# P·V products of 256 columns, a reordered output projection with kept weights, and a second block group in the down projection

## The chip, the cores and the metric

The kernel runs on one core of a Trainium2 chip. The metric is device time in microseconds (us): 2593.43 is the median of three runs of the kernel before (2592.44 to 2593.51). PE is the matrix engine (TensorE), PEld its weight loads, DVE the vector engine, ACT the scalar engine, POOL the gpsimd engine, SP the queue that issues most loads.

## What is computed

A trunk of two layers on 16 learned and 1024 input frames (T = 1040), width 1024, everything in float32:

```python
for i in range(DEPTH):
    xn = rms_norm(h, attn_norm[i])
    gq, gk, gv, gr, glr, fq, fk, fv, ff = split(xn @ w_in[i])
    o_gla = rms_norm(gla_chunk_causal(gq / 8, gk, gv, log_a), gla_norm[i]) * silu(gr)
    o_fox = rms_norm(forgetting_attention(fq, fk, fv, log_f), fox_norm[i])
    h = h + concatenate([o_gla, o_fox]) @ w_out[i]
    h = h + conv_ffn(rms_norm(h, ffn_norm[i]), w_up[i], conv_w[i], conv_b[i], w_down[i])
return rms_norm(h, final_norm)[:, 16:]

def conv_ffn(x, w_up, conv_w, conv_b, w_down):
    u, g = split(causal_conv3(x @ w_up, conv_w) + conv_b)
    return (silu(g) * u) @ w_down
```

`forgetting_attention` is a causal softmax attention with eight heads of 64 columns and a bias from a cumulated forget gate. The gated width D_FF is 22 tiles of 128.

## The kernel before

The hidden state stands transposed: eight tiles of 128 features by 1040 frames. PE multiplies in a 32-bit format with a shorter fraction, so each operand is split into a high part (ACT casts it) and a low part (DVE subtracts), and one product takes three matmuls (`mm3`, lines 218 to 220). The split of weights is `weights` (L179 loads, L185 is the caller of the cast `hi`, L187 the subtraction `lo`) and, for block products, `up_split` (L1028, L1029); that of activations is L332 and L333.

A layer has these stages. *Attention* (forget-gate heads, `fox`): queries go in groups of one or two tiles of 116, keys in tiles of 116 too. For each pair of key chunk and query tile the exponentials P are transposed on PE (`fox_transposes`, L690) into one bank, split into `PT` (high and low part beside each other for each of four key tiles), and `fox_av` (L708) multiplies them by V: one matmul per key tile and part, 232 columns wide for two query tiles and 116 on the diagonal. Products of the next head's projections fill PE in between.

*Output projection* (`wout` in `ffn_up`): the frames are done in two halves `h` of 520 (layer 1: 524 and 516), each in 36 x 2 x 3 = 216 matmuls; eight output tiles `m` in the orders (4, 0, 5, 1, 6, 2, 7, 3) and (0, 4, 1, 5, 2, 6, 3, 7). Tiles 0 to 3 were done for seven of the eight inputs during attention, so they take 6 matmuls and tiles 4 to 7 take 48. Banks rotate over four pairs by `i % 4`. Weights are loaded and split one tile ahead, once for each half. Each tile's result is added to the residual h (DVE, L1110), squared (ACT, L1116) and summed into `acc` (DVE, L1117). `scale` sums `acc` over partitions with a matmul by ones into a bank `ssq` of pair 3 (L1086), which DVE reads (L1089), and makes the factor of the norm (`rsqrt`, L273 to L277). In the second half, after the second tile, `scale(0)` and then the normed operands of the up projection are made among the remaining tiles (L1094, L1052, L1053); `gt` and `dd` (L1121, L1123) are the scaled differences between halves.

*Up projection*: block products with seven instead of eight multiplications on 2 x 2 blocks (weights by input halves and output tiles, activations by frame halves), in the order of the list `seq`; numbers p = 1 to 7 name the products, which share banks a, x and y and accumulate on them.

*Down projection* (`ffn_down`): the 22 gated tiles come back from DRAM (`actd`) and go in groups, `GROUPS` and `LAST`. A group "n" or "r" is plain: for eight output tiles, two halves, its tiles, two column pieces of 260 (layer 1: 256), three matmuls. "n" copies the result to a buffer `do` (ACT, L1462) and adds it to `hm` in DRAM by an accumulating DMA of POOL (L1464); "r" adds it on DVE to residual tiles that `load_residual` has loaded from `hm` (L1435). A group "s" is done by seven block products (`down_blocks`), for four pairs j of output tiles, in the order 2, 6, 5, 7, (j+1's 1), 4, 3 behind the first: bank a is copied by ACT after products 1, 6, 7 and 4 (L1376), x and y are added by DVE (L1375), and the sums `du` and `dg` go to `hm` by accumulating DMA (L1390, L1394). `prepare` is a generator that loads, splits and combines the operands of coming groups; `pump` takes steps of it between products while enough buffers ("slots" of 1040 columns, first in, first out) are free. *Last group* (`down_last`): three gated tiles in column chunks of 400, 384 and 256 over eight single banks; its result is added to the residual (L1538), squared, and is the next layer's input.

PE's order is that of the program in the stages behind attention; all other engines, and PE in attention, are ordered by a scheduler. Waits are in order on each engine, and on SP's and POOL's queues.

## Time and profile before

| | us |
|---|---|
| median of three runs | 2593.43 |
| the profiled run | 2591.4 |
| its span, first to last instruction | 2589.6 |
| output projection, layer 0 (first matmul to the first of the up projection) | 538.9 to 600.9 |
| up projection, layer 0 | 600.9 to 1048.1 |
| down projection, groups, layer 0 | 1048.1 to 1258.6 |
| last group of layer 1, final norm | 2537.3 to 2589.6 |

The trace is of one execution. A row of a timeline has start and duration (us), engine, line, operation, output<-inputs, shape, count, and in brackets how long the engine was idle before it and what ended that. A row of a group has the count, the busy time and the mean duration in ns, then the idle time before its instructions and who ended it. Matmuls overlap, so what one costs is the distance between starts, not the duration.

### The profile page before, as it was taken

The numbers are of one execution on the slowest core, as the hardware profiler recorded it, in microseconds if no ns is written. First come the engines' busy times: TensorE is split into PE (matmuls) and PEld (weight loads), VectorE is DVE, ScalarE is ACT, GpSimd is POOL, SyncE is SP. The second block draws the span as 40 slices with busy tenths as digits, with TensorE's granted clock in tenths as the row PEclk, the third lists the DMA queues.
The fourth block names the chain that finished last, engine by engine and source line by source line (L and its number), as shares of the span: only waits on it lengthen the run. The fifth ranks groups of instructions, "written<-read, shape, count | busy, mean of one in ns | idle before, by whom it ended". The sixth has DMA issues, their size and how long they took to land.

```text
span 2589.6 us, 48743 instructions
## 1 busy us (share of the span) xinstructions
PE 2495.7 (96%) x19278; PEld 2424.9 (94%) x19278; DVE 1786.6 (69%) x3494; ACT 1288.4 (50%) x2745; POOL 432.6 (17%) x598
## 2 busy tenths in 40 slices
PE   8999999898999999999999999999999999999997
PEld 7988999898999999999999899998899999999997
DVE  7656776759877777853665666776697777777535
ACT  7336666635544445641443565665464444455312
POOL 4033334310000000100301233332100000001002
PEclk9999999999999999999999999999999999999998
DMA  3132134342322223863312222143423222257721
GB/s 125 65 89 60 51 93 127 109 145 89 110 75 87 79 79 129 200 165 107 110 50 67 72 78 76 57 146 114 148 70 114 78 74 86 76 162 179 196 61 67
DMA packets 119670, 263.03 MB, mean 102 GB/s; under 512 B 15008, under 2 KB 32672, under 8 KB 119440
## 3 DMA queue, kind: packets, MB, share of 16 engines
q1 hardware_dynamic: 95136, 184.89, 22.8%
q0 software_dynamic: 22432, 72.71, 10.1%
q8 instruction: 151, 2.47, 0.4%
q10 hardware_dynamic: 1872, 2.31, 0.3%
q14 instruction: 79, 0.65, 0.1%
HBM read 179.26 MB, written 67.81 MB: 95 GB/s over the span
## 4 chain that ended last, share of the span: by engine, by line
PE 62%; issue 16%; DVE 13%; ACT 4%; DMA 3%; POOL 1%; SPq 0%; DVEq 0%; POOLq 0%; ACTq 0%
PE mm L218 7%; PE mm L220 6%; PE mm L219 6%; PE up L218 5%; PE up L219 5%; PE up L220 5%; PE down L218 5%; PE down L219 5%; PE down L220 5%; PE av L708 2%; DVE S L657 2%; PE tr L690 2%; ACT P L669 1%; PE wo L218 1%; PE wo L219 1%
## 5 line engine op out<-in xcount | busy, mean ns | idle before, releaser
L218 PE MATMUL up<-x,hi 128*128 128x260 f32 (+1 forms) x2464 | 697.3, 283 | 2.3 <-ACT x L1052 1.6
L220 PE MATMUL up<-x,hi 128*128 128x260 f32 (+1 forms) x2464 | 695.8, 282 | 2.2 <-DVE x L1053 2.2
L219 PE MATMUL up<-x,lo 128*128 128x260 f32 (+1 forms) x2464 | 696.1, 283 | 0.8 <-DVE lo L1029 0.8
L220 PEld LDWEIGHTS up<-x,hi 128*128 128x128 f32 x2464 | 465.5, 189 | 3.1 <-DVE x L1053 3.1
L218 PEld LDWEIGHTS up<-x,hi 128*128 128x128 f32 x2464 | 464.4, 188 | 3.4 <-ACT x L1052 2.2
L219 PEld LDWEIGHTS up<-x,lo 128*128 128x128 f32 x2464 | 464.8, 189 | 1.0 <-DVE lo L1029 1.0
L1029 DVE TENSOR_TENSOR lo<-raw,hi 128x512 fp32r<-128x512 f32 x364 | 249.0, 689 | 171.3 <-ACT hi L1028 171.3
L218 PE MATMUL mm<-xh,hi 128*128 128x348 f32 (+4 forms) x1056 | 364.6, 345 | 0.0
L220 PE MATMUL mm<-xl,hi 128*128 128x348 f32 (+4 forms) x1056 | 340.1, 322 | 0.0
L219 PE MATMUL mm<-xh,lo 128*128 128x348 f32 (+4 forms) x1056 | 339.2, 321 | 0.0
L1028 ACT CAST hi<-raw 128x512 fp32r<-128x512 f32 x364 | 224.5, 620 | 145.0 <-PE up L220 87.4
L185 ACT CAST hi<-raw 128x512 fp32r<-128x512 f32 (+2 forms) x192 | 112.4, 587 | 201.4 <-PE down L220 114.2
L218 PEld LDWEIGHTS mm<-xh,hi 128*128 128x128 f32 x1056 | 200.2, 190 | 5.9 <-issue 5.3
L219 PEld LDWEIGHTS mm<-xh,lo 128*128 128x128 f32 x1056 | 200.1, 190 | 0.4 <-issue 0.3
L220 PEld LDWEIGHTS mm<-xl,hi 128*128 128x128 f32 x1056 | 198.9, 188 | 0.3 <-issue 0.3
L219 PE MATMUL down<-ah,lo 128*128 128x260 f32 (+1 forms) x704 | 198.6, 282 | 0.3 <-DVE lo L187 0.3
L220 PE MATMUL down<-al,hi 128*128 128x260 f32 (+1 forms) x704 | 198.3, 282 | 0.0
L218 PE MATMUL down<-ah,hi 128*128 128x260 f32 (+1 forms) x704 | 198.3, 282 | 0.0
L669 ACT ACTIVATE P<-S,m 116x460 f32<-116x460 f32 (+2 forms) x224 | 124.8, 561 | 100.1 <-DVE m L657 97.9
L333 DVE TENSOR_TENSOR PT<-tr,PT 116x464 fp32r<-116x464 f32 (+3 forms) x240 | 123.0, 516 | 63.2 <-ACT PT L332 62.3
L1222 POOL DMA_DIRECT2D actd<-cv x44 | 23.6, 535 | 763.5 <-DVE cv L1221 742.5
L1011 DVE TENSOR_TENSOR raw<-raw,raw 128x512 f32<-128x512 f32 x198 | 129.9, 689 | 22.4 <-DMA raw<-in_wd_dram 18.4
(276 smaller groups left out, 5901.0 us busy)
## 6 DMA issues: line engine op xcount, KB each, us to landing
raw<-in_wm_dram SPq DMA_DIRECT2D x338, 256.0 KB, 2.8
raw<-in_wd_dram SPq DMA_DIRECT2D x64, 256.0 KB, 3.5
actd<-cv POOLq DMA_DIRECT2D x22, 520.0 KB, 3.0
actd<-cv POOLq DMA_DIRECT2D x22, 512.0 KB, 3.0
cb<-cd SPq DMA_DIRECT2D x16, 520.0 KB, 3.8
st<-actd SPq DMA_DIRECT2D x14, 520.0 KB, 4.8
st<-actd SPq DMA_DIRECT2D x14, 512.0 KB, 5.3
kA<-kA SPq DMA_DIRECT2D x24, 260.0 KB, 4.3
```

The costliest lines, as they stand in the source:

```text
L185: nc.scalar.copy(hi[:, :n, :], raw[:, :n, :])
L218: nc.tensor.matmul(ps, wh, xh[:, c0:c0 + n], start=first, stop=False, skip_group_check=more)
L219: nc.tensor.matmul(ps, wl, xh[:, c0:c0 + n], start=False, stop=False, skip_group_check=more)
L220: nc.tensor.matmul(ps, wh, xl[:, c0:c0 + n], start=False, stop=last, skip_group_check=more)
L333: nc.vector.tensor_tensor(out=lo, in0=src, in1=hi.bitcast(F32), op=ALU.subtract)
L657: nc.vector.tensor_tensor_reduce(out=S[:rows, :n], in0=S[:rows, :n], in1=cb[:rows, c0:k1], scale=1.0, scalar=(BIG if ci == 0 else m[:rows, ...
L669: nc.scalar.activation(P[:rows, :n], S[:rows, :n], AF.Exp, scale=-1.0, bias=m[:rows, nch - 1:nch], accum_out=(den if nch == 1 else d3[:row ...
L690: nc.tensor.transpose(tr[:w, j, :rows], P[:rows, o:o + w], id_)
L708: nc.tensor.matmul(av[:, a:width], w.rearrange("p a b -> p (a b)"), x, start=(t == 0 and i == 0), stop=(t == last and i == 1))
L1011: nc.vector.tensor_tensor(out=q[out][:, :nk, :], in0=q[a][:, :nk, :], in1=q[b][:, :nk, :], op=op)
L1028: nc.scalar.copy(hi[:, :nk, :], src[:, :nk, :])
L1029: nc.vector.tensor_tensor(out=lo[:, :nk, :], in0=src[:, :nk, :], in1=hi[:, :nk, :].bitcast(F32), op=ALU.subtract)
```

## The change

Five edits stand together.

1. `GROUPS`: the third group is "n" instead of "r", the fourth "s" instead of "r". So four more gated tiles (15 to 18) go by block products, and residual tiles are loaded late: those of output tiles 6 and 7 after product 7 of the third pair, the others behind the block products. In the last pair the sums are added on DVE to the residual instead of by DMA.
2. Sums of block products get four buffers of their own that rotate (`outgoing`), held over the whole block group; `pump` no longer keeps slots free for them. The first weights of the last group are loaded and split during the last block products.
3. P·V: the four key tiles of a chunk stand in reversed order and the parts apart, so that a matmul of 256 columns reads 24 columns of the tile next to it, into columns of the bank that nobody reads.
4. Output projection: the banks of the second half go (0, 1, 2, 0, 1, 3, 2, 1); the split weights of tiles 5 and 6 are kept from the first half to the second, in buffers of the up projection's pool.
5. In the second half the squares of the last two tiles aren't added by DVE but summed by PE, in four more matmuls by ones.

```diff
-GROUPS, LAST = (("n", 0, 3), ("s", 3, 8), ("r", 11, 4), ("r", 15, 4)), (19, 3)
+GROUPS, LAST = (("n", 0, 3), ("s", 3, 8), ("n", 11, 4), ("s", 15, 4)), (19, 3)
...
-            nc.tensor.transpose(tr[:w, j, :rows], P[:rows, o:o + w], id_)
-        self.split(PT[ci][:w, :nt, 0, qs], PT[ci][:w, :nt, 1, qs], tr[:w, :nt, :rows])
+            nc.tensor.transpose(tr[:w, 3 - j, :rows], P[:rows, o:o + w], id_)
+        at = slice(4 - nt, 4)
+        self.split(PT[ci][:w, 0, at, qs], PT[ci][:w, 1, at, qs], tr[:w, at, :rows])
...
+        ts = list(range(4 * part, min(4 * part + 4, last + 1)))
+        if part == 0 and last:
+            ts[:2] = 1, 0
+        for t in ts:
+            a, b = 0 if t <= tiles[0] else FT, width
...
+                    r, p = self.rows_of(t), 3 - t % 4
+                    w, x = q["V"][e][:r, t, :, :], PT[part][:r, i, p, a:width]
+                    if a == 0 and p < 3:
+                        b = 256
+                        x = PT[part][:r, i].rearrange("p a b -> p (a b)")[:, 2 * FT * p:2 * FT * p + b]
+                nc.tensor.matmul(av[:, a:b], w.rearrange("p a b -> p (a b)"), x,
...
             ps, r = bank2("ssq", 3), acc[:, sl[h]]
+            parts = [r] + [half(sq, i) for i in range(2) if h]
             for c in range(2):
-                nc.tensor.matmul(ps[:, c, :n], self.ones[:], acc[:, halves[h] + c * n:halves[h] + c * n + n],
-                                 start=True, stop=True)
+                for i, x in enumerate(parts):
+                    nc.tensor.matmul(ps[:, c, :n], self.ones[:], x[:, c * n:c * n + n],
+                                     start=i == 0, stop=i == len(parts) - 1)
...
-                ps = bank2("wo", i % 4)
+                ps = bank2("wo", (0, 1, 2, 0, 1, 3, 2, 1)[i] if h else i % 4)
...
-                    nc.vector.tensor_tensor(out=acc[:, sl[h]], in0=acc[:, sl[h]], in1=t, op=ALU.add)
+                    if not (h and i >= KD - 2):
+                        nc.vector.tensor_tensor(out=acc[:, sl[h]], in0=acc[:, sl[h]], in1=t, op=ALU.add)
...
+        keep = {5: (fw, [("raw2", 7)] * 2), 6: (fw, [("hi2", 3), ("lo2", 3)])}
...
+            w = self.weights(self.wm[lyr, M_WO + m][:, KD - 1 if m < NSPLIT else 0:KD, :], keep=keep.get(m))
+            if m in keep:
+                kept[m] = w
...
+        def out(j, m, t):
+            if residual and j == NP - 1:
+                h = residual(m)[:, o0:T]
+                nc.vector.tensor_tensor(out=h, in0=t[:, o0:T], in1=h, op=ALU.add)
+            else:
+                nc.gpsimd.dma_start(self.hm[m][:, o0:T], t[:, o0:T], accum_op=ALU.add)
+        ring = []
+        def outgoing():
+            if not ring:
+                ring.extend(s.get(F32, "do") for _ in range(4))
+            ring.append(ring.pop(0))
+            return ring[-1]
...
-                q["u"] = s.get(F32, "du")
+                q["u"] = outgoing()
...
+                if residual and (j, p) == (NP - 2, 7):
+                    residual(KD - 1), residual(KD - 2)
...
-                    self.pump(1, 3)
+                    self.pump(1)
                 elif j and p == 5:
-                    self.pump(1, 4)
+                    self.pump(1)
+            s.put(*ring)
...
+                    more = (lambda t=then: len(ahead) < 2 and fetch(t)) if then else \
+                        (lambda: len(self.last_w[0]) < 2 and self.last_weight(lyr, ids))
...
-            if not hT:
-                load_residual()
+            for k in range(KD):
+                residual(k)
```

How the instructions move shows at three places; rows of the changed kernel bear its own line numbers. The first is DVE in the second half of the output projection, layer 0, from the residual sum of output tile 6 on: `h<-wo` are residual sums (h_5939 is output tile 6, h_5936 tile 3), `r<-r,sq` the sum of squares, `lo` a weight split, `x` a low part for the up projection. Before:

```order
L1110 TENSOR_TENSOR h_5939<-wo,h_5939 128x520
L1053 TENSOR_TENSOR x_7525<-h_7065,x_7523 128x520
L1123 SCALAR_TENSOR_TENSOR dd<-h_5939,vec,gt 128x520
L1117 TENSOR_TENSOR r<-r,sq 128x520
L1053 TENSOR_TENSOR x_7520<-h_5933,x_7518 128x520
L187 TENSOR_TENSOR lo<-raw,hi 128x512 x2
L1110 TENSOR_TENSOR h_5936<-wo,h_5936 128x520
```

Now, from the residual sum of output tile 1 (h_5934) on, at the place of the norm's factor (`nt`, `r<-nt`):

```order
L1124 TENSOR_TENSOR h_5934<-wo,h_5934 128x520
L191 TENSOR_TENSOR lo<-raw,hi 128x512
L1041 TENSOR_TENSOR lo<-raw,hi 128x512
L279 SCALAR_TENSOR_TENSOR nt<-nt 128x520
L1133 TENSOR_TENSOR r<-r,sq 128x520
L280 TENSOR_TENSOR nt<-nt 128x520
L1023 TENSOR_TENSOR raw_7713<-raw,raw_7713 128x512
L281 SCALAR_TENSOR_TENSOR r<-nt 128x520
```

Before, both halves of the last 48-matmul tile's weights (x2) stood behind tile 6's sum; now one of them (L191) and two operations for up-projection weights (L1041, L1023) stand ahead of the factor. The other half stands three rows ahead of tile 3's sum, where it stood right before it.

The second place is ACT at the end of the first block group of layer 0: `do` copies of sums, `ah` and `x` casts of operands for the groups that follow. Now:

```order
L336 CAST ah<-st 128x1040
L189 CAST hi<-raw 128x512
L336 CAST x_14350<-st 128x1040
L336 CAST x_14380<-st 128x1040
L1424 COPY do<-down 128x520
L336 CAST ah<-st 128x1040
L189 CAST hi<-raw 128x512
L336 CAST x_14413<-t_14411 128x1040
L336 CAST x_14444<-st 128x1040
L1424 COPY do<-down 128x520
L336 CAST x_14510<-st 128x1040
```

The first copy is that after product 6 of the last pair, the second that after product 7. Casts named `x` are operands of the second block group and have no counterpart before; there casts `ah` of plain operands stood between these copies.

The third is SP at the end of the second block group of layer 0; `hm_101` to `hm_108` are output tiles 0 to 7, 128x384 the last group's weights. Now:

```order
L180 DMA raw<-in_wd_dram 128x384
L1484 DMA h_15512<-hm_102 128x1040
L180 DMA raw<-in_wd_dram 128x384 x4
L1484 DMA h_15516<-hm_104 128x1040
L1484 DMA h_15514<-hm_103 128x1040
L180 DMA raw<-in_wd_dram 128x384
L1484 DMA h_15520<-hm_106 128x1040
L1484 DMA h_15518<-hm_105 128x1040
L1484 DMA h_15510<-hm_101 128x1040
L180 DMA raw<-in_wd_dram 128x384 x2
```

Before, all eight residual loads stood ahead of the plain groups' last weights, far from the last group; now six of them stand among the last group's weights, tile 0 last, and the weights of output tiles 6 and 7 behind it.

More of the change, by code (lines that the diff above doesn't have):

```diff
@@ L699, in fox_av @@
         width = FT * (len(tiles) - 1) + self.rows_of(last)
-        for t in range(4 * part, min(4 * part + 4, last + 1)):
-            a = 0 if t <= tiles[0] else FT
+        ts = list(range(4 * part, min(4 * part + 4, last + 1)))
[3 more added lines that the diff above has]
+            a, b = 0 if t <= tiles[0] else FT, width
             for i in range(2):
@@ L1130, in f, with wout_weights @@
                     first_operand(k)
-            return (self.wm[lyr, M_WO + m][:, k0:KD, :], f)
-        self.stream([wout(i, h) for h in range(2) for i in range(KD)])
+            return f
+        keep = {5: (fw, [("raw2", 7)] * 2), 6: (fw, [("hi2", 3), ("lo2", 3)])}
+        kept = {}
+        def wout_weights(h, i):
+            m = orders[h][i]
+            if m in kept:
+                return kept.pop(m)
+            w = self.weights(self.wm[lyr, M_WO + m][:, KD - 1 if m < NSPLIT else 0:KD, :], keep=keep.get(m))
+            if m in keep:
+                kept[m] = w
+            return w
+        todo = [(h, i) for h in range(2) for i in range(KD)]
+        ahead = wout_weights(*todo[0])
+        for this, nxt in zip(todo, todo[1:] + [None]):
+            w, ahead = ahead, nxt and wout_weights(*nxt)
+            wout(this[1], this[0])(w)
         for x in mix:
@@ L1351, in pump, with down_blocks @@
             n -= 1
[L1353 removed]
+    def down_blocks(self, lyr, g0, ng, X, pp, fw, halves, after, residual=None):
         nc, s = self.nc, self.slots
@@ L1429, in ffn_down, with residual @@
         two = lambda ap: ap.rearrange("p (a b) -> p a b", b=n)
-        hT, ahead, going = [], [], []
-        def load_residual():
-            for k in range(KD):
-                hT.append(s.get(F32, f"h{k}", first=ids))
+        hT, ahead, going = [None] * KD, [], []
+        def residual(k):
+            if hT[k] is None:
+                hT[k] = s.get(F32, f"h{k}", first=ids)
                 nc.sync.dma_start(hT[k][:, o0:T], self.hm[k][:, o0:T])
+            return hT[k]
         def complete(done):
@@ L1507, in run @@
                 ahead.clear()
-            if not hT:
-                load_residual()
+            for k in range(KD):
+                residual(k)
             complete(lambda: all(j in acts for j in range(LAST[0], sum(LAST))))
@@ L1518, in ffn_down, with last_weight @@
         return tail, run
+    def last_weight(self, lyr, es):
+        w, held = self.last_w
+        m, (g0, ng) = len(w), LAST
+        if m % 2 == 0:
+            held += [self.slots.get(F32R, "wl", (128, 2, 4, 128), es) for _ in range(2)]
+        w.append(self.weights(self.wd[lyr, m][:, g0:g0 + ng, :], [x[:, m % 2, :, :] for x in held[-2:]]))
     def down_last(self, lyr, hT, pp, dchunks, acts, at_end, es):
@@ L1523, in down_last @@
         g0, ng = LAST
[L1524 to L1529 removed]
+        while len(self.last_w[0]) < KD:
+            self.last_weight(lyr, es)
+        (w, held), self.last_w = self.last_w, ([], [])
         nxt = at_end()
```

32 lines of the change are left out of this document (11 added, 21 removed).

## Prediction

> **What bounds the kernel now.** I read the page's busy times first, then its stages as windows, then the timeline of PE at each place that the change touches.
>
> ```profile
> span 2589.6 us, 48743 instructions
> PE 2495.7 (96%) x19278; PEld 2424.9 (94%) x19278; DVE 1786.6 (69%) x3494; ACT 1288.4 (50%) x2745; POOL 432.6 (17%) x598
> ```
>
> PE is the bound: 2589.6 - 2495.7 = 94 us of the span are free of it. So a change pays by fewer or shorter matmuls, or by removing a wait of PE. The windows (us, busy time and count of PE, PEld, DVE, ACT, POOL, granted clock, DMA) show where another engine sets the pace:
>
> ```profile
> 538.00:601.00 63.00, 56.79 (x440) 55.71 (x439) 45.54 (x76) 29.44 (x54) 9.21 (x17) 0.95 0.48 146
> 601.00:700.00 99.00, 96.08 (x790) 94.76 (x789) 95.06 (x137) 57.65 (x89) 5.40 (x8) 1.00 0.32 99
> 1048.00:1262.00 214.00, 211.47 (x1750) 210.84 (x1749) 116.09 (x155) 76.38 (x119) 14.43 (x17) 1.00 0.55 144
> 1262.00:1292.00 30.00, 30.00 (x192) 30.00 (x192) 23.35 (x40) 18.59 (x40) 17.49 (x17) 1.00 0.34 122
> 571.00:580.00 9.00, 7.14 (x43) 6.84 (x43) 6.71 (x11) 4.37 (x8) 1.08 (x2) 0.81 0.52 160
> 580.00:590.00 10.00, 9.53 (x80) 9.32 (x79) 9.73 (x17) 5.78 (x12) 1.08 (x2) 1.00 0.36 117
> 590.00:601.00 11.00, 7.79 (x54) 7.58 (x54) 11.00 (x19) 6.51 (x12) 1.08 (x2) 0.84 0.31 111
> ```
>
> In layer 0 the first is the output projection, the second the head of the up projection, the third the down projection by groups, the fourth its last group, the last three the end of the output projection. In the down projection PE is full and DVE is half idle: only fewer matmuls help there. From 590 to 700 DVE is full: there PE's waits are DVE's backlog. For a matmul's price I take the distance of starts (ends overlap); 24 steps lie between the first and second row, and between the third and fourth:
>
> ```profile
> 1079.75 0.28 PE L220 MATMUL down<-al,hi 128*128 128x260 f32 x1
> 1082.63 0.29 PE L220 MATMUL down<-al,hi 128*128 128x260 f32 x1
> 2349.79 0.28 PE L219 MATMUL down<-ah,lo 128*128 128x256 f32 x1
> 2352.62 0.28 PE L219 MATMUL down<-ah,lo 128*128 128x256 f32 x1
> ```
>
> So 0.120 us at 260 columns and 0.118 at 256.
>
> **Second block group.** Four gated tiles done plainly take 8 x 2 x 4 x 2 x 3 = 384 matmuls a layer, as seven products 4 x 7 x 2 x 2 x 3 = 336. Both layers save 96 x 0.12 = **11.5 us**. Against it stand waits that the first block group already shows (both layers by column count, then places in layer 0):
>
> ```profile
> L218 PE MATMUL down<-x,hi 128*128 128x260 f32 x224 | 63.5, 284 | 2.5 <-ACT dg L1376 1.4 <-ACT du L1376 1.2
> L218 PE MATMUL down<-x,hi 128*128 128x256 f32 x224 | 63.3, 282 | 3.0 <-ACT du L1376 1.4 <-ACT dg L1376 1.3 <-DVE dg L1375 0.3
> 1100.83 0.39 PE L218 MATMUL down<-x,hi 128*128 128x260 f32 x1 [0.68 <-ACT dg L1376]
> 1155.22 1.06 ACT L332 CAST ah<-st 128x1040 fp32r<-128x1040 f32 x1 [0.37 <-DMA st<-actd]
> 1154.89 1.24 DVE L333 TENSOR_TENSOR al<-st,ah 128x1040 fp32r<-128x1040 f32 x1 [2.00 <-ACT ah L332]
> 1156.19 0.58 ACT L1376 COPY du<-down 128x520 f32<-128x520 f32 x1
> 1156.67 2.21 ACT L332 CAST ah<-st 128x1040 fp32r<-128x1040 f32 x2
> 1156.83 0.39 PE L218 MATMUL down<-x,hi 128*128 128x260 f32 x1 [1.17 <-ACT du L1376]
> ```
>
> Product 4 follows product 7 directly in the first and last pair of output tiles and accumulates on the bank that ACT is copying: 0.68 each, so 1.4 a layer again. A product now lasts 12 x 0.12 = 1.44 us instead of 2.9, so it covers half as much. The ring of four buffers adds a wait: the third pair's second output reuses the buffer of the second pair's first, whose accumulating DMA started four products (5.8 us) earlier.
>
> ```profile
> hm<-dg POOLq DMA_DIRECT2D x4, 520.0 KB, 5.7
> hm<-du POOLq DMA_DIRECT2D x4, 520.0 KB, 6.4
> h<-hm SPq DMA_DIRECT2D x8, 520.0 KB, 5.0
> ```
>
> With 0.7 for the DVE add and 6.4 to landing, ACT's copy there starts 1.3 late; the product behind it covers 1.44 of 0.8 + 1.3, so PE waits about 0.7. Waits on DVE's add (0.3 in layer 1's row) I put at 1 a layer. Together 3.1, so 6 for both, and the group nets **-5.5**. Bounds: no new wait, -11.5; twice these waits, +1. In the first block group the same ring is covered, since four products there last 11.5.
>
> **Hand-over to the last group.** The residual tiles now load behind the block group, h of output tile 0 last, after SP has waited for the sums of the third pair. The last of these is complete six products (8.6 us) before the end, its DMA starts 0.8 later and lands 6.4 after that, 1.4 before the end; three loads at 5.0 bring tile 0 some 4 to 5 us after it. DVE stands at tile 0's add then, with weight splits for tiles 6 and 7 behind it; PE needs those after six tiles, and eight banks hold eight. At 9 matmuls a tile, 192 in 30 us give 9 x 0.156 = 1.4 us a tile, so 8.4 us. Price 0; if the load comes later than 8, each us costs one. DVE's two added residual sums (1.24 us each by row 1154.89, of the same size) fit into 30 - 23.35.
>
> **At nothing.** The first of the later plain groups now sends its sums by accumulating DMA instead of adding to residual tiles. Its 16 copies a layer (0.58, row 1156.19) lie on ACT beside 384 matmuls, 46 us; POOL issues eight more of these DMAs, each of which has three output tiles (17 us) for its 6.4 to landing. If that cover were gone, each late buffer would hold PE by what exceeds 17. The reversed order of the transposes in their bank, and so of the casts behind, changes neither their number nor size. The kept weights save four loads a layer, which no wait of PE rests on once the split is on time. They hold four of the seven raw buffers until the second half's fourth tile, so the up projection's second set of loads starts some 14 us ahead of its use instead of earlier; 5.0 to 6.4 for a load of twice the size (rows above) is covered.
>
> **P·V.** Key tiles other than 0, 4 and 8, up to the first of the two query tiles, are widened: 6 + 4 + 3 + 1 = 14, times two (high, low part), eight heads and two layers. So 448 matmuls go from 232 columns to 256.
>
> ```profile
> 209.24 1.14 PE L708 MATMUL av<-PT,V 116*128 116x232 f32 x8
> 210.21 0.46 PE L690 MATMUL tr<-ident,P 116*116 116x116 f32 x3
> 214.84 0.83 PE L708 MATMUL av<-PT,V 112*128 112x232 f32 x6
> 215.51 0.37 PE L654 MATMUL S<-kA,qA 128*116 128x460 f32 x1
> ```
>
> Eight take 0.97 (0.121 each), six 0.67 (0.112). At 256 columns 0.118 is the price, so the wider form gains nothing: between 448 x (0.118 - 0.121) = -1.3 and 448 x 0.006 = +2.7. I take **+2.5**, since most runs are as the second. The Trainium skill's page "TensorE: Matmul & The Clock Gate", "Back-to-back issue gap", speaks against this edit more strongly: columns / 2.4 + 2.5 ns gives 99 and 109 ns, +4.6 us in all. The rows show less, since 232 columns already cost 112.
>
> **Output projection.** The timeline of layer 0:
>
> ```profile
> 571.43 1.04 PE L1086 MATMUL ssq<-r,ones 128*128 128x260 f32 x4
> 572.12 0.47 PE L218 MATMUL wo<-mh,hi 128*128 128x260 f32 x1
> 575.05 0.36 PE L218 MATMUL wo<-mh,hi 128*128 128x260 f32 x1 [1.86 <-DVE nt L1089]
> 576.77 0.42 PE L218 MATMUL wo<-mh,hi 128*128 128x260 f32 x1
> 577.42 0.42 PE L218 MATMUL wo<-mh,hi 128*128 128x260 f32 x1
> 593.82 0.59 PE L219 MATMUL wo<-mh,lo 128*128 128x260 f32 x1 [3.21 <-DVE lo L187]
> ```
>
> 432 matmuls x 0.12 + 0.7 (two ssq) are 52.5 of the stage's 62, so 9.5 are lost. The first wait, 1.86, is for the bank in which ssq stands until DVE has read it; the new order of banks gives that product another. Behind it matmuls start 0.65 / 3 = 0.217 apart: half rate for some 15, 1.5 us. The second, 3.21 and another half-rate stretch, is for a weight split late in DVE's queue. What DVE does:
>
> ```profile
> 576.28 0.70 DVE L275 SCALAR_TENSOR_TENSOR nt<-nt 128x520 f32<-128x520 f32 x1 [0.57 <-ACT nt L274]
> 580.26 0.69 DVE L187 TENSOR_TENSOR lo<-raw,hi 128x512 fp32r<-128x512 f32 x1 [1.32 <-ACT hi L185]
> 593.07 1.30 DVE L187 TENSOR_TENSOR lo<-raw,hi 128x512 fp32r<-128x512 f32 x2
> 641.86 1.31 DVE L1053 TENSOR_TENSOR x<-h,x 128x520 fp32r<-128x520 f32 x2
> ```
>
> An operation is worth 0.6 (two in 1.30, overlapping by 0.1). Kept weights remove four splits, three of them in the full stretch, and the squares on TensorE two adds: 5 x 0.6 = 3.0. The waits of 0.57 (for ACT's exponent) and 1.32 (for weights that are now kept) are filled: the first half of the last tile's split and two operations of the up projection stand ahead of them now. So DVE reaches any point of its backlog 4.9 earlier. PE could gain 9.5 less four more ssq calls (0.35 each, 1.4), so 8, but it then meets the operands of the up projection:
>
> ```profile
> L218 PE MATMUL up<-x,hi 128*128 128x260 f32 x123 | 35.2, 286 | 1.2 <-ACT x L1052 1.2
> L220 PE MATMUL up<-x,hi 128*128 128x260 f32 x122 | 34.6, 283 | 1.1 <-DVE x L1053 1.1
> ```
>
> PE waits for DVE here already (601 to 650). So it keeps what DVE gains: 5 a layer, **-10**; the 1.4 of ssq lies in the waits that PE has left. Bounds: the removed operations alone, less the ssq calls, -1.6 x 2 = -3; PE's full 8, -16. The Trainium skill, same page, "What's actually happening", sets a clock gate by a free-running window of 3.4 us; the half rate after a wait of 1.86, which ends by 580, agrees.
>
> **Sum.** The profiled run took 2591.4: -10 + 2.5 - 5.5 = -13 gives 2578.4. The median of the runs is 2.0 above it, so 2580.4; I say **2581**.
>
> **The rivals.**
> - The backlog doesn't bind: DVE's later work gives way and PE keeps all 8 a layer: 2593.4 - 16 + 2.5 - 5.5 = 2574. For it: the four waits of PE in the up head are short (2.3 in all). Against it: DVE is full up to 700. Chance 0.17.
> - The block group pays nothing: its 56 products of 1.44 expose 0.1 us more each, 5.5 in all: 2593.4 - 10 + 2.5 = 2586. Half-long products speak for it; DVE at 54% in that stage against. 0.22.
> - The output projection gives it all back: DVE's order puts up-projection work ahead of the splits, and only the block group counts, -5.5 + 2.5 with -1: 2589. 0.10.
> - Slower: the operands of the second group are made in the last pair of the first. Seven casts of 1.06 for them and the four subtractions and sums of DVE that feed them stand between ACT's copies of the sums, and a cast waits for a slot that a product still reads. If each of four products there waits a product's length (2.9) for its copy, that is 23 in both layers: 2593.4 - 13 + 23 = 2603. Row 1156.83 shows one such wait of 1.17. Against it: the casts between the copies of products 6 and 7 (three of 1.06 and one of 0.6) fit into two products (5.8). It decides from (13 + 5.2) / 8 = 2.3 a product on. 0.11.
> - The forecast has 0.40.
>
> **Numbers.** The range 2570 to 2593 takes in all but the slow rival and the ends. About 0.2% (5.2 us) is what a measurement of this kernel can tell from no change. Faster holds the forecast, the first two rivals less 0.05: 0.74. Same: the third and that 0.05: 0.15. Slower: 0.11.
>
> **What would show it.** Right: no wait of PE on ssq's bank, the wait of 3.21 under 1.5, waits of PE in the up head grown from 2.3 to about 5, av at 0.118, block group with waits near 3 a layer. Wrong: PE waits for casts or copies in the first group's last pair, a wait at the start of the last group, or up head waits unchanged (then the first rival).

## The result, and the profile after

The changed kernel took 2594.85 us (median of 12 runs, 2588.83 to 2601.75), the kernel before 2595.11 beside it (12 runs, 2592.04 to 2600.93). The ratio is 0.9996, 95% interval 0.9985 to 1.0007: no change, and outside the predicted range of 2570 to 2593. The page's head of the changed kernel, whose profiled run took 2594.69:

```profile
span 2592.9 us, 48884 instructions
PE 2501.4 (96%) x19198; PEld 2427.7 (94%) x19198; DVE 1790.8 (69%) x3532; ACT 1328.4 (51%) x2847; POOL 456.9 (18%) x626
```

PE was to get shorter by 96 matmuls and by its waits; its busy time rose by 5.7 us instead. The windows (columns as in the prediction) of the output projection, the head of the up projection and the groups of the down projection in layers 0 and 1 show where:

```profile
532.00:586.00 54.00, 52.94 (x435) 52.51 (x436) 36.64 (x62) 22.11 (x43) 10.02 (x17) 1.00 0.54 166
586.00:685.00 99.00, 96.55 (x774) 95.01 (x773) 94.54 (x136) 59.01 (x92) 4.88 (x7) 0.98 0.31 94
1036.00:1254.00 218.00, 207.91 (x1684) 206.24 (x1683) 117.71 (x169) 97.93 (x167) 26.32 (x31) 0.98 0.71 162
2318.00:2541.00 223.00, 207.50 (x1690) 205.77 (x1689) 116.17 (x168) 96.92 (x167) 26.53 (x31) 0.97 0.69 158
```

The output projection fell from 62.0 to 54.1 us (538.9 to 600.9 before, 532.0 to 586.1 now), DVE's busy time in these windows from 45.5 to 36.6. Attention ended at 532 instead of 538.9. But the groups of the down projection, though they have 48 matmuls fewer, grew: from their first matmul to the first of the last group, in layer 0 from 210.5 to 217.8, in layer 1 from 208.7 to 221.9, at a granted clock of 0.98 and 0.97 where it was 1.00. Of a lead of 11.6 us at the start of layer 0's down projection 4.3 are left at its end; in layer 1 a lead of 9.8 becomes a lag of 3.3. The groups of PE's matmuls there that head a product (layer 0, then layer 1; idle time before them at the end):

```profile
L222 PE MATMUL down<-x,hi 128*128 128x260 f32 x336 | 97.7, 291 | 9.2 <-ACT do L1424 8.8 <-DVE do L1423 0.5
L222 PE MATMUL down<-x,hi 128*128 128x256 f32 x336 | 97.9, 291 | 15.5 <-ACT do L1424 14.4 <-DVE do L1423 1.1
```

Before, these waits were 2.5 and 3.0. PE waits for ACT's copies of sums (L1424, which the change has made of L1376). The timeline of ACT, and PE's row behind each, shows what the copies stood behind, at one place for each of three causes:

```profile
2363.07 1.04 ACT L336 CAST ah<-st 128x1024 fp32r<-128x1024 f32 x1 [8.72 <-DMA st<-actd]
2364.02 0.58 ACT L1424 COPY do<-down 128x512 f32<-128x512 f32 x1
2364.65 0.58 PE L222 MATMUL down<-x,hi 128*128 128x256 f32 x1 [3.03 <-ACT do L1424]
...
2509.97 0.51 ACT L189 CAST wl<-raw 128x384 fp32r<-128x384 f32 x1 [3.14 <-DMA raw<-in_wd_dram]
2510.39 0.58 ACT L1424 COPY do<-down 128x512 f32<-128x512 f32 x1
2511.02 0.38 PE L222 MATMUL down<-x,hi 128*128 128x256 f32 x1 [1.79 <-ACT do L1424]
...
2524.99 0.59 ACT L1424 COPY do<-down 128x512 f32<-128x512 f32 x1 [6.15 <-DMA hm<-do]
2525.63 0.58 PE L222 MATMUL down<-x,hi 128*128 128x256 f32 x1 [4.42 <-ACT do L1424]
```

A (first rows): the cast of a later group's activations waits 8.72 us for its load, and the copy waits in line. B: the cast of the last group's weights waits for their load. C: the copy itself waits for its rotating buffer, whose accumulating DMA has not landed. ACT takes its work strictly in order; the Trainium skill says so of ACT and DVE ("Perfetto Trace Analysis", "Tensor Engine Instruction (MATMUL, LD_WEIGHTS)"), and these rows agree.

A long wait costs more than itself. Take one in the last pair of the first block group, where cause A has company. ACT there in layer 1, ahead of the copy for which PE waits 3.11 us (its row is the first of the fence after):

```profile
2430.39 1.05 ACT L336 CAST ah<-st 128x1024 fp32r<-128x1024 f32 x1 [1.97 <-DMA st<-actd]
2433.86 1.04 ACT L336 CAST x<-st 128x1024 fp32r<-128x1024 f32 x1 [0.95 <-DVE st L1346]
2434.81 0.58 ACT L1424 COPY do<-down 128x512 f32<-128x512 f32 x1
```

One cast waits 1.97 for its load, another, for the second group, 0.95 for a sum of DVE, and with two more casts in between these take some 3.8 us themselves. PE behind that wait:

```profile
2435.45 0.39 PE L222 MATMUL down<-x,hi 128*128 128x256 f32 x1 [3.11 <-ACT do L1424]
2435.67 0.28 PE L223 MATMUL down<-x,lo 128*128 128x256 f32 x1
2435.79 0.29 PE L224 MATMUL down<-x,hi 128*128 128x256 f32 x1
2435.90 0.39 PE L222 MATMUL down<-x,hi 128*128 128x256 f32 x1
2436.09 0.41 PE L223 MATMUL down<-x,lo 128*128 128x256 f32 x1
2436.31 0.41 PE L224 MATMUL down<-x,hi 128*128 128x256 f32 x1
```

From the fourth row on the starts are 0.21 apart instead of 0.12. So it was behind all five waits of 2.7 us or more in the two stages, for 12 to 27 matmuls, 9.3 us together (each slow step less 0.12); behind the waits of up to 1.8 there were one or two such steps. What brings it on, the last section says. The sum for layer 1 then nearly closes: waits of 15.5 on the row above against 3.0 before, slow steps worth 5.6 against 0.5, less 48 matmuls x 0.12 = 5.8, make 11.8; measured 13.2.

### The profile page after: what moved, and what is told of

It is laid out like the page before. It is cut to its first block, busy times and chain, and to the rows that moved or that the text cites. A ratio compares the mean times of both kernels' runs of the same rounds, so it can differ in the third digit from the quotient of the medians.

```text
span 2592.9 us, 48884 instructions
## 1 busy us (share of the span) xinstructions
PE 2501.4 (96%) x19198; PEld 2427.7 (94%) x19198; DVE 1790.8 (69%) x3532; ACT 1328.4 (51%) x2847; POOL 456.9 (18%) x626
## 4 chain that ended last, share of the span: by engine, by line
PE 71%; DVE 13%; issue 6%; ACT 5%; DMA 4%; POOL 1%; SPq 0%; DVEq 0%; ACTq 0%; POOLq 0%
PE up L222 9%; PE up L224 9%; PE up L223 9%; PE mm L222 6%; PE mm L223 6%; PE mm L224 6%; PE down L222 4%; PE down L223 4%; PE down L224 4%; PE av L720 2%; DVE S L661 2%; PE tr L694 2%; ACT P L673 1%; DMA st<-actd 1%; DVE x L1065 1%
## 5 line engine op out<-in xcount | busy, mean ns | idle before, releaser
L1041 DVE TENSOR_TENSOR lo<-raw,hi 128x512 fp32r<-128x512 f32 (+1 forms) x420 | 271.0, 650 | 222.1 <-ACT hi L1040 219.1
L1040 ACT CAST hi<-raw 128x512 fp32r<-128x512 f32 (+1 forms) x420 | 246.8, 592 | 164.2 <-PE up L224 94.5
L222 PE MATMUL down<-x,hi 128*128 128x260 f32 (+1 forms) x672 | 195.6, 291 | 24.7 <-ACT do L1424 23.1
L224 PE MATMUL down<-x,hi 128*128 128x260 f32 (+1 forms) x672 | 193.5, 288 | 0.0
L223 PE MATMUL down<-x,lo 128*128 128x260 f32 (+1 forms) x672 | 193.5, 288 | 0.0
L1023 DVE TENSOR_TENSOR raw<-raw,raw 128x512 f32<-128x512 f32 (+1 forms) x230 | 142.4, 647 | 38.4 <-DMA raw<-in_wd_dram 26.3
L222 PEld LDWEIGHTS down<-x,hi 128*128 128x128 f32 x672 | 131.3, 195 | 27.8 <-ACT do L1424 25.8
```

What stands on the lines that cost most here:

```text
L222: nc.tensor.matmul(ps, wh, xh[:, c0:c0 + n], start=first, stop=False, skip_group_check=more)
L223: nc.tensor.matmul(ps, wl, xh[:, c0:c0 + n], start=False, stop=False, skip_group_check=more)
L224: nc.tensor.matmul(ps, wh, xl[:, c0:c0 + n], start=False, stop=last, skip_group_check=more)
L1023: nc.vector.tensor_tensor(out=q[out][:, :nk, :], in0=q[a][:, :nk, :], in1=q[b][:, :nk, :], op=op)
L1040: nc.scalar.copy(hi[:, :nk, :], src[:, :nk, :])
L1041: nc.vector.tensor_tensor(out=lo[:, :nk, :], in0=src[:, :nk, :], in1=hi[:, :nk, :].bitcast(F32), op=ALU.subtract)
```

## The experiments

Medians in us. e1 to e4 were run beside the kernel before at a median of 2595.11, e5 to e8 at 2594.90, e9 to e12 at 2596.59. The last column is the length of the down projection's groups in layers 0 and 1 in the profiled run (210.5 and 208.7 before).

| run | time | ratio to before, 95% | groups in the profile |
|---|---|---|---|
| the changed kernel | 2594.85 | 0.9985 to 1.0007 | 217.8, 221.9 |
| e1: second block group undone | 2578.66 | 0.9923 to 0.9948 | 216.6, 215.4 |
| e2: P·V edit alone | 2578.66 | 0.9921 to 0.9949 | 211.7, 208.3 |
| e3: output projection alone | 2587.22 | 0.9959 to 0.9984 | 210.0, 209.2 |
| e4: P·V layout at 232 columns | 2596.18 | 0.9993 to 1.0014 | 211.0, 207.2 |
| e5: P·V at 248 columns | 2596.67 | 0.9988 to 1.0012 | 210.8, 208.9 |
| e6: output projection and P·V | 2570.72 | 0.9879 to 0.9917 | 211.6, 207.7 |
| e7: changed, three suspects gone | 2574.92 | 0.9901 to 0.9937 | 209.7, 209.5 |
| e8: changed, with the pump's reserve | 2584.60 | 0.9933 to 0.9969 | 217.1, 216.6 |
| e9: changed, last weights late | 2594.93 | 0.9979 to 1.0001 | 216.4, 219.2 |
| e10: changed, six rotating buffers | 2578.16 | 0.9908 to 0.9938 | 211.4, 210.0 |
| e11: e7 and a new order | 2565.73 | 0.9863 to 0.9895 | 208.1, 202.2 |
| e12: e11, last weights loaded early | 2571.97 | 0.9881 to 0.9914 | 211.3, 204.4 |

**Which edit did what (e1, e2, e3, e6).** e1 sets the table of groups back:

```diff
-GROUPS, LAST = (("n", 0, 3), ("s", 3, 8), ("n", 11, 4), ("s", 15, 4)), (19, 3)
+GROUPS, LAST = (("n", 0, 3), ("s", 3, 8), ("r", 11, 4), ("r", 15, 4)), (19, 3)
```

> The changed kernel with the third and fourth group of the down projection plain again (GROUPS as before, kind r); P-V, output projection, the rotating buffers of the one block group and the pump without reserve stay. Theory G (the second block group loses 13 us in layer 0 and 19 us in layer 1 to waits of PE for ACT's copies, more than the 11.5 us its fewer matmuls save): the lead of about 10 to 11 us that the changed kernel has at the start of each layer's down projection is kept in both layers, so about 18 to 22 us under the kernel before (ratio 0.992 to 0.993), groups of the down projection 208 to 212 us long. Rival N (the changed kernel's early lead is an accident of one execution, or the time goes in the last group and the next layer): within 5 us of the kernel before.

It took 2578.66, 16 us less than the changed kernel, where theory G has 18 to 22 under the kernel before. But its groups are 216.6 and 215.4 us long where 208 to 212 were expected: waits of 3.65 us in layer 0 and of 3.17 and 3.71 in layer 1 stayed in the first block group. So G held in part. e2 is the kernel before with edit 3, e3 with edits 4 and 5, e6 with all three.

> The kernel before with the P-V edit alone (reversed layout, products of 256 columns). Theory S (the other order of the bank and of the program lets the scheduler place transposes, casts and products of attention so that PE waits less): attention of layer 0 about 5 to 7 us shorter, the whole 7 to 11 us faster than before. The prediction's price: 2.5 us slower. Rival O (attention was shortened by another edit of the changed kernel): same as before or 2.5 us slower.

> The kernel before with the edits of the output projection alone (order of banks, kept weights, squares summed on PE). The prediction: 10 us faster (5 a layer), output projection 8 us shorter in each layer and the up projection 2 to 3 us longer. Rival: given back in the up projection or behind, within 5 us of before.

> The kernel before with the P-V edit and the output projection's edits, and its own down projection. If the two gains add up (16.5 and 8 us): 2570 to 2572, ratio 0.9905. If the buffers and the pump of the changed down projection cost nothing where no second block group stands, it is the same as e1_plain_groups, 2578.7.

P·V alone gave 16.5 us, the opposite of its predicted price. The output projection gave 7.9. Together they gave 24.2, so they add up. What stands between e6 and the changed kernel, 24.1 us, is the price of edits 1 and 2. By the medians about 8 of it are for the buffers and the pump without a second block group (e1 less e6; e1 loads its residual tiles where the kernel before does), 16 for the second group.

The profiles divide it otherwise: e1's groups are 12.7 us longer than e6's, the changed kernel's 7.6 longer than e1's. The rest of the second group's 16 is mostly in the next stretch, from the last group of layer 0 to the end of layer 1's attention: 557.5 us in the changed kernel, 551.0 in e1. There the changed kernel waits 2.7 us more at the head of layer 1 (see the hand-over, below) and has two stretches of half rate of 3.4 us, each of which costs 1.7, where e1 has none. e6, with ACT and DVE in the same order in that attention, has three, so such stretches come and go without an edit, and a few us between two runs need not lie where the edit is. By the groups' length about half of the 24 belongs to edit 2 alone.

**Why P·V got faster (e4, e5).** e4 leaves the wide read away, e5 makes it 248 columns:

```diff
-                        b = 256
+                        b = 248
```

> The kernel before with the reversed layout and order of the P-V edit, but its products left at 232 columns. Theory S: as e2_pv_only or 2 to 4 us faster still (448 products at 0.112 instead of 0.120 are 3.6 us less). Rival W (the width itself shortens attention): same as the kernel before.

> e2_pv_only with its wide products cut from 256 to 248 columns, so that 16 columns of the neighbour are read instead of 24. The scheduler then puts PE in the order of the kernel before again (0 places differ in attention) and ACT too, but for 4 places; e2_pv_only had 100 places differing on ACT. Theory O (the 17 us of e2_pv_only come from the order in which the scheduler puts ACT and DVE once a product is 256 wide, not from the width on the chip): the 1.38 us wait of the transposes for PT comes back in each head, and the time is that of the kernel before, 2594 to 2598. Rival W (reading wide products or the bank past 232 columns helps by itself): near e2_pv_only, 2579 to 2583.

Neither is faster than before. e4 has the kernel before's order on PE, ACT and DVE without one difference, and its time. So neither the layout nor 16 more columns matter; at 256 the scheduler chose another order, which shows at some 100 places each on ACT and DVE in the whole program and at 20 on PE in attention of layer 0. The timelines of ACT, DVE and PE at one of these, e4 first:

```profile
238.75 0.55 ACT L669 ACTIVATE P<-S,m 116x344 f32<-116x344 f32 x1 [1.65 <-DVE m L657]
239.29 0.54 ACT L332 CAST PT<-tr 116x464 fp32r<-116x464 f32 x1
239.86 0.64 DVE L333 TENSOR_TENSOR PT<-tr,PT 116x464 fp32r<-116x464 f32 x1 [1.14 <-ACT PT L332]
240.56 0.61 PE L690 MATMUL tr<-ident,P 116*116 116x116 f32 x4 [1.38 <-DVE PT L333]
```

and e2, the same work:

```profile
234.60 0.53 ACT L332 CAST PT<-tr 116x464 fp32r<-116x464 f32 x1
235.02 0.55 ACT L669 ACTIVATE P<-S,m 116x344 f32<-116x344 f32 x1
236.54 0.27 PE L655 MATMUL S<-kL,qA 128*116 128x228 f32 x1
236.65 0.56 PE L690 MATMUL tr<-ident,P 116*116 116x116 f32 x4
```

In e4 the cast of PT, behind which DVE's subtraction frees the bank that PE's next transposes want, stands behind an exponential that waits for DVE's row maximum. In e2 the cast goes first, and PE does not wait. The transposes' idle time from 180 to 532 us, in e4, e5 and e2:

```profile
L690 PE MATMUL tr<-ident,P 116*116 116x116 f32 (+1 forms) x352 | 62.5, 268 | 10.2 <-DVE PT L333 10.2
...
L690 PE MATMUL tr<-ident,P 116*116 116x116 f32 (+1 forms) x352 | 62.4, 268 | 9.9 <-DVE PT L333 9.6
...
L690 PE MATMUL tr<-ident,P 116*116 116x116 f32 (+1 forms) x352 | 61.6, 266 | 3.8 <-DVE PT L333 3.8
```

In layer 0 that is 6.4 us; attention as a whole got 6.1 shorter than e4's, and the stretch from the last group of layer 0 to the end of layer 1's attention 5.6. The other runs agree: before all transposes of a layer's attention PE is idle 6.7 to 8.4 us in the ten profiles with the new order, 13.3 to 15.0 in the four with the old, in each layer. These profiles account for 11 to 12 of the 16.5 to 17.5 us: e2's profiled run, 2582.5, was its slowest of six. The rest lies in runs without a trace and stays open. That order and not width is the cause is shown at 232 and 248 columns; 232 columns in the new order were not run.

**What the block group's waits hang on (e7 to e10).** e8, e9 and e10 each take one suspect away, e7 all three:

```diff
-                    self.pump(1)
-                elif j and p == 5:
-                    self.pump(1)
+                    self.pump(1, 3)
+                elif j and p == 5:
+                    self.pump(1, 4)
...
-                        (lambda: len(self.last_w[0]) < 2 and self.last_weight(lyr, ids))
+                        (lambda: None)
...
-                ring.extend(s.get(F32, "do") for _ in range(4))
+                ring.extend(s.get(F32, "do") for _ in range(6))
```

> The changed kernel with its block group, but with three suspects taken away at once: six rotating buffers instead of four, the pump again leaves 3 and 4 slots free in block groups, and the last group's weights are loaded and split only when that group begins. Theory G (PE's waits in the down projection, some 11 us in layer 0 and 17 us in layer 1, hang on these): groups of the down projection 206 to 210 us long in both layers, the whole 2568 to 2578. Rival T (the waits come from the added traffic of accumulating DMAs, which stays): 2590 to 2597.

> The changed kernel, with only the pump's reserve of 3 and 4 slots put back in block groups. Theory A (without the reserve a load of activations gets a slot that was just released, comes late, and ACT stands at its cast in front of a copy of sums): the waits of 3.6 us in layer 0 (at the first block group's tail) and 3.0 and 3.1 us in layer 1 fall to about 1.2, the whole 6 to 9 us under the changed kernel, 2586 to 2589. Rival: same as the changed kernel, 2592 to 2598.

> The changed kernel, with only the early load and split of the last group's weights taken back. Theory B (a cast of these weights waits on ACT for its load, with copies of sums queued behind it): the waits of PE of 2.7 us in layer 0 and 1.8 us in layer 1 in the second block group go, and 1 to 1.5 a layer come back at the start of the last group, so 1 to 4 us under the changed kernel, 2591 to 2594. Rival (the hand-over was worth what it was meant to be): 2595 to 2600.

> The changed kernel, with only the rotating buffers raised from four to six. Theory C (the third pair's second sum waits on ACT for the accumulating DMA of the second pair's first): the wait of PE of 4.4 us in layer 1 and the 0.35 in layer 0 go, 4 to 6 us under the changed kernel, 2589 to 2591. Rival (six buffers take two slots from the pump, loads of activations come later still): 2594 to 2600.

e7 gave 20 us, so the traffic of the accumulating DMAs, which stays, is not the cause of these. It only brings the groups back to e6's length (209.7 and 209.5 against 211.6 and 207.7): the second group's saving is still eaten. e8 gave 10.3: the waits of 3.62, 3.03 and 3.11 became 1.50, 2.50 and 1.43, though a new one of 2.10 came in layer 0. In its profile the groups are 0.6 and 5.3 us shorter, 5.9 of the 10.1 between the two profiled runs; the rest lies in other stages, so only some 6 are shown to be the reserve's. e9 gave nothing. Its waits for the weights went (2.74 and 1.79), but in layer 0 ACT then came to the third pair's copy sooner and waited there instead:

```profile
1236.59 0.59 ACT L1424 COPY do<-down 128x520 f32<-128x520 f32 x1 [5.92 <-DMA hm<-do]
1237.23 0.38 PE L222 MATMUL down<-x,hi 128*128 128x260 f32 x1 [4.13 <-ACT do L1424]
```

In the changed kernel PE waited 0.35 us there. So in layer 0 B had hidden C. From the start of layer 0's down projection to the next output projection it was 1.9 us slower than the changed kernel (1034.9 to 1812.0 against 1036.5 to 1811.7); in layer 1, where C stood beside B already, it won 2.3 from the start of the down projection to the end (2318.8 to 2590.7 against 2318.7 to 2592.9). e10 gave 16.7, three times what was expected, and its groups show why (PE's rows as above, where L1513 is the copy of the plain groups, L1462 before; then ACT's casts of activations in layer 0, of the changed kernel last):

```profile
L222 PE MATMUL down<-x,hi 128*128 128x260 f32 x336 | 95.7, 285 | 8.0 <-ACT do L1424 5.5 <-ACT do L1513 2.4
L222 PE MATMUL down<-x,hi 128*128 128x256 f32 x336 | 95.8, 285 | 7.5 <-ACT do L1424 5.4 <-ACT do L1513 1.5 <-DVE do L1423 0.6
L336 ACT CAST ah<-st 128x1040 fp32r<-128x1040 f32 x7 | 7.4, 1062 | 10.6 <-DMA hm<-do 5.6 <-DMA st<-actd 2.0 <-PE down L223 1.6
...
L336 ACT CAST ah<-st 128x1040 fp32r<-128x1040 f32 x7 | 7.4, 1064 | 20.2 <-DMA st<-actd 10.0 <-DMA hm<-do 7.4 <-PE down L223 2.8
```

The ring's wait went as expected. But the two slots that it takes are also slots that the pump doesn't have, so the casts of cause A moved out of the block group too: their waits for loads fell from 10.0 to 2.0. In layer 1 the rows of SP in the changed kernel show why the load of A was late, with ACT's cast for which it is:

```profile
2332.10 21.31 SPq L1013 DMA_DIRECT2D raw<-in_wd_dram  x6
2353.51 0.58 SPq L1292 DMA_DIRECT2D st<-actd  x1
...
2363.07 1.04 ACT L336 CAST ah<-st 128x1024 fp32r<-128x1024 f32 x1 [8.72 <-DMA st<-actd]
```

Six weight loads take 21 us to issue, since they wait for their buffers; the load of activations follows at 2353.51, 0.8 us before ACT came to the cast. It then took 9.5 us to land (2363.04), where the median of its line is 4.1; from 2353 to 2364 the DMA engines were busy all the time (share 1.04). So a late issue and a slow landing add up in that wait. Fewer steps of the pump in the block group, by a reserve or by fewer free slots, keep these casts out of it.

**A better version (e11, e12).** Two kinds of wait were chosen from those left in e7: 0.68 us where product 4 directly follows 7 on the same bank, and a cast that waits for the plain group's buffers, the first to come free. e11 changes both:

```diff
-        seq = [(0, 1), (0, 2), (1, 1), (0, 6), (0, 5), (0, 7), (0, 4), (0, 3)]
+        seq = [(0, 1), (1, 1), (0, 6), (0, 5), (0, 7), (0, 2), (0, 4), (0, 3)]
         for j in range(1, NP):
-            seq += [(j, 2), (j, 6), (j, 5), (j, 7)] + ([(j + 1, 1)] if j + 1 < NP else []) + [(j, 4), (j, 3)]
+            seq += [(j, 2), (j, 6), (j, 5), (j, 7), (j + 1, 1)] if j + 1 < NP else [(j, 6), (j, 5), (j, 7), (j, 2)]
+            seq += [(j, 4), (j, 3)]
...
-                s.put(*going)
-                going.clear()
                 for j in range(g0, g0 + ng):
                     s.put(*acts.pop(j))
+                s.put(*going)
+                going.clear()
```

> e7_group_mended with two more edits. First, in the first and last pair of a block group product 2 goes between products 7 and 4, so that no product accumulates on a bank that ACT is just copying; this should take away the eight waits of 0.68 (0.84 with the half rate behind), 6.7 us in all. Second, the buffers of the plain group go back behind its operands, so that the first cast behind it does not wait for an accumulating DMA (3.5 us in layer 1, 1.6 in layer 0). If both hold: 2574.9 - 6.7 - 5 = 2563. If product 2 only moves the wait to DVE's add of bank y: 2568 to 2572.

> e11_order_puts, with the last group's first two weights loaded early but split only behind the last product but two, when they have landed. If the waits of 1.4 us at the start of the last group go and no cast stands on ACT for its load: 2 to 4 us under e11_order_puts. Rival (the cast still meets its load): same or 2 us more.

e11 is the fastest of all, 2565.73. Its waits, by the same rows:

```profile
L222 PE MATMUL down<-x,hi 128*128 128x260 f32 x336 | 95.9, 286 | 3.8 <-DVE do L1424 3.1 <-ACT do L1425 0.7
L222 PE MATMUL down<-x,hi 128*128 128x256 f32 x336 | 95.1, 283 | 2.0 <-DVE do L1424 2.0
```

(L1424 is DVE's sum here, L1425 ACT's copy.) That is near the 3 us a layer of the prediction. Against e6 it is 5 us less (2570.72 less 2565.73), near the -5.5 of the prediction. But the two intervals overlap, and e6 lacks the new order, which serves its first block group too: that the second group pays is likely, how much is not shown. e12 issues the loads of the last group's first weights, in the program, two or three products ahead of their casts, and lost 6 us (these intervals overlap too; its groups are 3.3 and 2.2 us longer): ACT met a load again.

```profile
1222.82 0.51 ACT L193 CAST wl<-raw 128x384 fp32r<-128x384 f32 x1 [5.12 <-DMA raw<-in_wd_dram]
1223.23 0.59 ACT L1429 COPY do<-down 128x520 f32<-128x520 f32 x1
```

The copy waits behind the cast as in the changed kernel. The cast's place in the program had moved towards the end, but this row is 24 us ahead of the last group (1247.1): the scheduler put it among the copies again.

## Why the prediction was wrong

**Second block group, -5.5: wrong, +24 (edits 1 and 2).** The saving stands (1680 matmuls in a layer's groups instead of 1728), and so do the small waits: 0.68 at each direct step from 7 to 4. The step that failed is the list of what it stands against: "waits that the first block group already shows". It took those waits as they were with the pump's reserve, and did not price `pump` without it; it took "in the first block group the same ring is covered" for the whole of edit 2 there. e1 against e6 puts 8 us on that, where no second block group stands, and 12.7 in the groups of the profiles. In the second block group the prediction had C at 0.7 us; 4.42 was measured in layer 1, and with B gone 4.13 in layer 0. The DMA in question, in layer 1:

```profile
2517.02 0.86 POOL L1410 DMA_DIRECT2D hm<-do  x1 [1.46 <-DVE lo L1041]
```

It was issued 2.9 us behind the product whose sum it carries, which ended at 2514.12, where 0.7 had been put for DVE's add, and took 7.9 us to land (2524.9) where 6.4 had been put. The two excesses, 2.2 and 1.5, are the difference between 0.7 and 4.42.

**The slower rival** had the kind of mechanism: casts of coming operands between ACT's copies. That its price of 23 us is near the measured 24.1 is luck. It put all of it on the last pair of the first group, and there the changed kernel shows waits of 3.62 and 3.11 and 3.2 of slow steps, 10 us; the rest lies elsewhere. It had the casts wait for a slot that a product reads; in that pair they waited for their loads (3.19 and 1.97) and for sums of DVE (0.95 each). It had been given 0.11, with the casts' own length (3.8 us, in two products of 5.8) as the argument against it. The argument counted how long casts run, not what they wait for.

**Hand-over, 0: wrong.** As forecast, PE waits for no residual tile in the last group, whose products eight banks hold. But the delay is not made good behind them. The first residual sum starts 4.2 us after that group's first matmul instead of 1.8, the sixteenth 31.0 instead of 25.9, and ACT comes to the cast of layer 1's first weights 38.5 instead of 35.4 us after it. There PE waits, and a stretch of half rate follows; the kernel before has no such wait:

```profile
1293.47 0.45 PE L222 MATMUL mm<-xh,wl 128*128 128x400 f32 x1 [1.94 <-ACT wl L189]
1294.67 0.45 PE L223 MATMUL mm<-xh,wl 128*128 128x400 f32 x1 [0.75 <-DVE wl L191]
```

All seven kernels with the second block group wait there, 1.7 to 4.7 us together; of the seven without it none waits more than 0.43. So the prediction looked for the price in the last group, and it stood one stage later. That it comes from the late residual tiles is argued, not shown: no run loads them early beside the second group. The weights of the last group that are loaded early neither cost nor won in the changed kernel: e9 without them took as long (2594.93), with waits of 1.41 and 1.35 at the start of that group and one of 4.34 instead of 1.94 at the head of layer 1.

**P·V, +2.5: wrong in sign, -16.5.** The price of the columns was right or a little low (the median distance of starts went from 0.112 to 0.120, 448 x 0.008 = 3.6; the 4.6 beside it is 448 x 10 ns = 4.5). The step that failed is under "at nothing": that the edit "changes neither their number nor size" was taken to leave the casts where they were. The number and the size stayed, but the order on ACT did not, and this order was worth more than all columns.

**Output projection, -10: right, but for another reason than the one given.** e3 measured 7.9 (2.1 less). The wait on ssq's bank went; the wait for the split fell from 3.21 to 1.04 us in layer 0, under the 1.5 named, and from 3.39 to 2.08 in layer 1, over it. In the profile after, the stage is 7.9 us shorter in layer 0 and 8.5 in layer 1, all that PE could gain, and the up projection 3.2 and 2.4 longer, which leaves 4.7 and 6.1 of the 5 a layer forecast. The step that failed is what was to take the rest back: waits for DVE in the up head were to grow from 2.3 to about 5. They were 1.0 for ACT and 1.5 for DVE there in layer 0 (1.2 and 1.1 before), which the prediction had named as the first rival's sign. What the up projection lost is half rate: slow steps worth 3.4 us in each layer instead of 0.9 and 1.0, and the four more matmuls by ones.

**The sum.** -8, -16.5 and +24 make no change, by accident: two of the three terms were wrong, by 19 and 30 us, with the hand-over in the last.

## What to carry to other kernels

Before a wait is costed, list what stands in line on the engine that ends it, and when each of these gets its data: a copy of 0.6 us behind a cast that waits for its load is as late as the load. A reserve of buffers can be what keeps a planner's loads and casts out of a tight stage; take it away only with that stage's in-order queues in view, and try such suspects together too, since one can hide another (e9). Where a scheduler orders engines, compare the order on all of them, not only on the one whose work changes: an edit that costs PE 2 to 4 us won 16.5 by another order of casts. And a delay that a stage hides can still be paid in the next: follow it until it is made good.

## What the runs showed of the hardware

Half rate comes in fixed windows. In the clock records of all 14 traces the stretches at a granted clock of 0.50 begin, within a trace, at whole multiples of 3.413 us from each other, and last one or two such windows (3.41 or 6.83 us); only the one that reaches to the program's end has another length. Two of the changed kernel's:

```profile
2435.92:2439.32 3.40, 3.40 (x19) 3.40 (x18) 3.40 (x5) 2.42 (x3) 0.00 (x0) 0.50 0.02 5
2524.67:2531.48 6.81, 5.85 (x27) 5.85 (x28) 2.20 (x5) 2.86 (x7) 0.86 (x1) 0.50 0.52 119
```

The length of a wait alone does not bring it on. It came behind one of 1.81 us (e11, layer 0), and not behind one of 2.76 (e10, layer 0):

```profile
1221.65 0.39 PE L222 MATMUL down<-x,hi 128*128 128x260 f32 x1 [1.81 <-DVE do L1424]
1222.10:1225.50 3.40, 3.40 (x18) 3.40 (x17) 1.52 (x4) 0.41 (x1) 1.06 (x2) 0.50 0.95 265
...
1226.34 0.39 PE L222 MATMUL down<-x,hi 128*128 128x260 f32 x1 [2.76 <-ACT do L1424]
1226.00:1232.00 6.00, 5.66 (x46) 5.66 (x47) 4.23 (x9) 3.42 (x9) 1.41 (x2) 1.00 0.30 72
```

What counts is how much of it falls into one window: all of the 1.81, but 1.71 and 1.05 of the 2.76. In the groups of the down projection of all 14 traces, the 21 windows at full rate in which PE was idle for 1.94 us or more were all followed by one at half rate, and of those with up to 1.79 none was; at 1.81 it came, at 1.84 it did not. That is a little over half a window. At the head of the up projection windows with 1.3 to 1.7 us of idle time were followed by half rate too, so the bound is that of the down projection alone. A window at half rate that PE fills costs it 1.7 us, half of 3.41.

The Trainium skill ("TensorE: Matmul & The Clock Gate", "What's actually happening") has a free-running window of about 3.4 us, and the multiples above agree. It lets the clock fall back after at least one idle window; here a window that was idle for somewhat more than half was enough.
